# Sixteen gate tiles as seven block products for eight, placed between the quarters of S5, with the gates kept in DRAM

## The chip, the cores and the metric

The kernel runs on one core of a Trainium2 chip. The metric is the device time of one execution in microseconds (us), the median over several runs. Engines: TensorE (PE; matmuls, with its weight loads as PEld), VectorE (DVE), ScalarE (ACT), GpSimd (POOL) and SyncE (SP). SP, ACT and POOL also issue DMA transfers, each through its own queue, and every engine works its instructions off in a fixed order.

## The reference

One decoder layer on x of 1024 tokens by 1024 channels, in float32. An S5 branch and an mLSTM branch read the same normalised x; gates from x weigh them, and their sum goes through a projection. Cross-attention and a gated FFN follow, which the change leaves alone.

```python
h  = rmsnorm(x, g)
u, q, k, v, o, i, f, gates = split(h @ w_in, IN_WIDTHS)   # gates: 2*D_MODEL = 2048 columns
ys = s5(u, ...)                                          # [1024, 512]
ym = mlstm(q, k, v, o, i, f, ...)                        # [1024, 512]
g  = sigmoid(gates + b_gate)
x  = x + (g[:, :D] * (ys @ w_br[0]) + g[:, D:] * (ym @ w_br[1])) @ w_out
# then cross-attention over 256 memory tokens, then the gated ConvFFN, then the last rmsnorm
```

## The kernel before, in words

Activations lie transposed: channels on the 128 partitions, 1024 tokens along a row. A float32 product is made of three float32r products: each factor is split into a high part (a cast on ACT, L186) and a low part (a subtraction on DVE, L187), and `gemm_part` (L214) does high by high, high by low and low by high. `ntile` loads one 512 KB block of weights for 128 output channels through SP's queue (WR), splits it (WH, WL) and runs 8 blocks of 128 channels by 3 products by 2 halves of the tokens, 48 matmuls of 128x512, into a PSUM tile M. A branch tile has 4 blocks of channels, 24 matmuls. `hx` holds the split x, scaled by the norm's gain; the norm's factor per token, `rb`, is multiplied in behind a product.

The order of the work is a list of steps by hand, `ORDER`, run through the loop `for step in ORDER`: `p`, `r` are the parameters and the run of a quarter of S5 (`s5_run`: transfers from Ud and Kd, L546 products, scans on DVE, L582/L583 products, L592 transposes, the result to Yd), `v` and `g` values and gate rows of the mLSTM, `j` a head's projections, `m` a head (`mlstm_head`; L731 to L774 are its products, its last step a power on POOL, L786, and transposes, L793), `s` splits a head's result (`ym_split`), `y` loads an S5 quarter, Gelu and split (`y_load`), `a` one gate tile and one branch tile of the mLSTM side. After the list come the glu tiles, the S5 side's gate and branch tiles (i=0), and then w_out. Instructions are placed by a scheduler that keeps to the data and the free buffers, so that filler from a neighbour step can stand between another step's instructions on PE.

`gate_tile(i, n)` is one `ntile` on `hx`, then a multiplication by `rb` (L800) and a sigmoid (L801); the tile gt lies in R, of which there are four buffers (`NR = 4`); rb holds one of them throughout. `merge_tile` multiplies it with the branch tile. `quad_sums(dst, src, jj, ...)` prepares the sums of weight blocks for products of the seven-for-eight kind that come later: on POOL's queue four DRAM-to-DRAM copies (L850), paced by the matmul that was last when the code was written out, and four adding transfers (L853), of which the third waits for the first, and the fourth for the third. `down_sums` (Dd) comes after every second S5 merge tile, `up_sums` (Uq) after `a5` and `a7` and later. `rstd_col(msq, D, rm)` behind w_out raises to a power on POOL (L242); PE uses rm at L1003. `psM`, `psA` give PSUM tiles M and A.

## Time and profile before

| what | value |
|---|---|
| median of three runs | 1622.83 us (1622.62 to 1624.99) |
| profiled execution | 1622.69 us, span 1620.9 us |
| mean granted clock of PE | 0.996 |
| DMA, mean | 144 GB/s; 233.83 MB |
| L800, DVE, 16 gate tiles | 19.6 us busy, 1222 ns each |
| L801, ACT, the sigmoids | 1154 ns each |
| gate weights, WR from w_in, 512 KB | 3.3 us to landing |

In a group's row of the profile stand line, engine, operation, output and inputs, shape and count; then the busy time, the mean of one in ns, the idle time of the engine just ahead and what ended it. In a row of a timeline the first two numbers are start and length in us, and the bracket gives the idle time ahead. In a row of waits stand the waiting engine, operation and line, what it waited for, the total in us, how often, and the longest.

### The profile page before, as it was taken

The page shows a single profiled execution, that of the slowest core. Times are in us where ns is not written, and L with a number is a line of the kernel's source. Part 1 is how long each engine was busy: PE and PEld are TensorE (multiplying, and loading weights), DVE is VectorE, ACT ScalarE, POOL GpSimd, SP SyncE. Part 2 cuts the span into 40 slices and gives each one's busy share as a digit, 9 for nine tenths or more (in the row PEclk, how much of TensorE's full clock was granted, in tenths as well). Part 3 has the DMA queues.
Part 4 walks back from the last instruction along what each step waited for, and adds up shares of the span by engine and source line. Part 5 has one row for each costly group of instructions (what it writes and reads, how often), then busy time and mean ns, then how long its engine had stood idle before and what let it go on. Part 6 is the DMA issues. An engine that isn't in the chain of part 4 may idle for free.

```text
span 1620.9 us, 20862 instructions
## 1 busy us (share of the span) xinstructions
PE 1597.7 (99%) x8031; PEld 1347.7 (83%) x8031; DVE 1056.6 (65%) x1698; ACT 700.7 (43%) x1153; POOL 144.1 (9%) x216
## 2 busy tenths in 40 slices
PE   9999999999999999999999999999999999999997
PEld 7898888888888888888888888888887888888887
DVE  7878767675344434344466468788889878867535
ACT  6446545633432223343354346444434445543423
POOL 0000000000111112100000000000111011221014
PEclk9999999999999999999999999999999999999998
DMA  5231211313665688953205244532677375886312
GB/s 198 95 97 57 79 53 59 86 46 104 175 156 149 161 252 240 292 132 107 97 29 206 104 156 163 198 108 78 190 183 196 109 181 172 309 284 207 119 39 105
DMA packets 87653, 233.83 MB, mean 144 GB/s; under 512 B 9601, under 2 KB 23617, under 8 KB 87553
## 3 DMA queue, kind: packets, MB, share of 16 engines
q1 hardware_dynamic: 58528, 138.73, 25.7%
q0 software_dynamic: 21488, 75.25, 18.7%
q10 hardware_dynamic: 7536, 18.52, 3.1%
q8 instruction: 63, 1.03, 0.3%
q14 instruction: 38, 0.30, 0.1%
HBM read 201.53 MB, written 85.46 MB: 177 GB/s over the span
## 4 chain that ended last, share of the span: by engine, by line
PE 93%; DVE 2%; issue 1%; DMA 1%; ACT 1%; SPq 0%; POOL 0%; POOLq 0%; DVEq 0%; ACTq 0%
PE M L214 41%; PE A L1208 14%; PE M L1208 10%; PE M L1352 6%; PE A L1352 5%; PE A L214 4%; PE M L299 1%; PE A L1074 1%; PE A L1020 1%; PE A L994 1%; PE M L614 1%; PE M L616 1%; PE M L615 1%; PE A L299 1%; DMA S<-in_w_up_dram 1%
## 5 line engine op out<-in xcount | busy, mean ns | idle before, releaser
L214 PE MATMUL M<-S,WH 128*128 128x512 f32 (+1 forms) x1704 | 459.6, 382 | 1.9 <-DVE dc L787 1.4
L214 PEld LDWEIGHTS M<-S,WH 128*128 128x128 f32 x1704 | 312.9, 188 | 63.0 <-issue 2.1
L214 PE MATMUL M<-S,WL 128*128 128x512 f32 (+1 forms) x884 | 277.5, 381 | 0.0
L186 ACT CAST WH<-WR 128x1024 fp32r<-128x1024 f32 (+2 forms) x107 | 99.4, 930 | 326.6 <-PE M L214 246.9
L214 PEld LDWEIGHTS M<-S,WL 128*128 128x128 f32 x884 | 165.8, 188 | 31.5 <-DVE WL L187 0.5
L187 DVE TENSOR_TENSOR WL<-WR,WH 128x1024 fp32r<-128x1024 f32 (+2 forms) x107 | 114.7, 1072 | 74.9 <-ACT WH L186 73.6
L1208 PE MATMUL M<-S,Y 128*128 128x512 f32 x468 | 112.2, 389 | 0.8 <-DVE Z L1221 0.8
L1208 PEld LDWEIGHTS M<-S,Y 128*128 128x128 f32 x468 | 87.8, 188 | 19.3 <-DVE Z L1221 1.1
L1231 DVE SCALAR_TENSOR_TENSOR S<-Z,cols,S 128x1023 f32<-128x1023 f32 (+1 forms) x72 | 90.8, 1278 | 7.2 <-ACT S L1229 7.2
L1208 PE MATMUL M<-S,W 128*128 128x512 f32 x324 | 78.3, 389 | 0.0
L186 ACT CAST W<-Y 128x512 fp32r<-128x512 f32 x51 | 31.4, 620 | 97.4 <-PE A L1208 67.4
L800 DVE TENSOR_TENSOR R<-M,R 128x1024 f32<-128x1024 f32 x16 | 19.6, 1222 | 82.6 <-PE M L214 82.6
L1208 PEld LDWEIGHTS M<-S,W 128*128 128x128 f32 x324 | 60.8, 188 | 12.6
L1208 PE MATMUL A<-S,W 128*128 128x512 f32 x288 | 70.6, 389 | 0.0
L1208 PEld LDWEIGHTS A<-S,W 128*128 128x128 f32 x288 | 54.1, 188 | 11.2
L1208 PE MATMUL A<-S,Y 128*128 128x512 f32 x240 | 60.1, 389 | 0.0
L1352 PE MATMUL M<-S,W 128*128 128x512 f32 x240 | 57.8, 389 | 0.0
L1208 PE MATMUL A<-R,W 128*128 128x512 f32 x228 | 56.5, 391 | 0.6 <-ACT Z L1215 0.5
L187 DVE TENSOR_TENSOR S<-S,S 128x512 fp32r<-128x512 f32 x79 | 51.8, 683 | 5.9 <-ACT S L186 5.8
L186 ACT CAST S<-S 128x512 fp32r<-128x512 f32 x79 | 46.4, 618 | 17.4 <-PE M L1352 6.1
L214 PE MATMUL A<-S,WH 128*128 128x512 f32 (+1 forms) x184 | 53.2, 372 | 0.5 <-ACT WH L186 0.5
L1208 PE MATMUL A<-VV,W 128*128 128x512 f32 x216 | 53.4, 389 | 0.0
(478 smaller groups left out, 3042.1 us busy)
## 6 DMA issues: line engine op xcount, KB each, us to landing
WR<-in_w_in_dram SPq DMA_DIRECT2D x29, 512.0 KB, 3.3
Uq<-in_w_uq_dram POOLq DMA_DIRECT2D x24, 512.0 KB, 9.0
Dd<-in_w_dq_dram POOLq DMA_DIRECT2D x24, 512.0 KB, 7.5
Td<-Gq POOLq DMA_DIRECT2D x24, 512.0 KB, 8.4
Gq<-S SPq DMA_DIRECT2D x18, 512.0 KB, 3.8
WR<-in_w_o_dram SPq DMA_DIRECT2D x16, 512.0 KB, 3.4
Y<-Uq SPq DMA_DIRECT2D x32, 256.0 KB, 3.9
S<-Td POOLq DMA_DIRECT2D x16, 512.0 KB, 5.4
```

The costliest lines, as they stand in the source:

```text
L186: A.copy(out=hi, in_=src)
L187: (lo_eng or V).tensor_tensor(out=lo, in0=src, in1=hi.bitcast(F32), op=ALU.subtract)
L214: last_mm[0] = PE.matmul(ps[:, s:e], lhsT, rhs[:, s:e], start=first and is_first, stop=last and is_last)
L299: PE.matmul(pus[j][h.start // 512], w_[:, 0, j * P : (j + 1) * P], x_[:, h], start=k == 0 and f, stop=k == KD - 1 and l)
L614: PE.matmul(ps, xh, wh, start=k == 0, stop=False)
L615: PE.matmul(ps, xh, wl, start=False, stop=False)
L616: PE.matmul(ps, xl, wh, start=False, stop=k == KD - 1)
L800: V.tensor_tensor(out=gt, in0=ps, in1=rb, op=ALU.mult)
L994: PE.matmul(pv[2 * m + j], lhsT, rhs[:, 0, 512 * j : 512 * j + 512], start=k == 0 and f, stop=k == KD - 1 and l)
L1208: up_mm[0] = PE.matmul(ps, lhsT[:, c], rhs, start=f, stop=l, skip_group_check=True)
L1231: V.scalar_tensor_tensor(out=acc[:, d_:], in0=raw[:, : T - d_], scalar=col("fcw", 3 * ct + 2 - d_), in1=acc[:, d_:], op0=ALU.mult, op1=ALU ...
L1352: paced[0] = PE.matmul(dps[p][n], lhsT[:, c], rhs, start=f, stop=l, skip_group_check=True)
```

## The change

Each group g of gates now covers four gate tiles (two of either side). Their 2x2 blocks of weights, the 2x2 blocks of x (even and odd blocks of channels, first and second half of the tokens) give seven products instead of eight. `gate_job(p, g)` does product p for group g, 24 matmuls; steps `e<p><g>` in ORDER. Products 2 and 3 are added on in the PSUM tile of the product that is ahead in their group (1 and 5, `gps[g]`); gu and gv keep partial results in VV and S. Weight sums are four `quad_sums` into Gw after `j0` to `j3`. The sums of x are `x_sums`: early (`A`, for product 6) and late (`B`, for 5, 7 and 4): xT is loaded again on POOL's queue into R, scaled on ACT, added on POOL (2 or 5 additions of 128x512) and split. A finished quarter goes through L800's multiplication and a sigmoid into DRAM `Gt` (ACT's queue), and `merge_tile` loads it again (SP's queue). The mLSTM result goes to DRAM `Ym` likewise and comes back in `ym_split`, now the last steps of the list. After the glu tiles the two sides' branch tiles alternate, 24 matmuls each.

```diff
@@ -48,14 +48,14 @@
 NPD = 9
 NPP = (NPD + 1) // 2
 NE = 8
-UP_SUMS_AT = ("a5", "a7")
 ORDER = (
-    "p0 r0 v0 p1 v1 g0 p2 r1 j0 m0 j1 m1 j2 m2 p3 s0 j3 m3 s1 s3 s2 y0 a0 a1 r2 a2 a3 r3 a4 y1 "
-    "y2 y3 a5 a6 a7 "
+    "p0 r0 v0 p1 v1 g0 p2 r1 j0 m0 j1 m1 j2 m2 p3 j3 m3 A0 A1 A2 A3 "
+    "e10 e11 e20 e21 r2 e12 e13 e22 e23 e60 e61 r3 B0 B1 B2 B3 e62 e63 "
+    "e70 e71 e72 e73 y0 y1 e40 e41 e42 e43 y2 y3 e50 e51 e30 e31 e52 e53 e32 e33 s0 s1 s2 s3 "
 ).split()
+GATE_SUMS_AT = {"j0": 0, "j1": 1, "j2": 2, "j3": 3}
+UP_SUMS_AT = {"e71": 0, "e52": 1}
 QKV = (
@@ -199,7 +199,10 @@
         else:
             hi, lo = alloc(F32R)[:, :fw], alloc(F32R)[:, :fw]
         wcount[0] += 1
-        split(hi, lo, raw, low[wcount[0] % 2])
+        if factor is None:
+            split(hi, lo, raw, low[wcount[0] % 2])
+        else:
+            scaled_split(raw, factor, hi, lo)
         return (hi.rearrange("p (k n) -> p k n", k=shape[0]),
                 lo.rearrange("p (k n) -> p k n", k=shape[0]))
@@ -302,6 +305,7 @@
     rb = R()
     Ud = dr.tile([GROUPS, CHG, BLK * NBLK], F32, name="Ud")
     Yd = dr.tile([4, P, T], F32, name="Yd")
+    Ym = dr.tile([NH, P, T], F32, name="Ym")
     Kd = dr.tile([GROUPS, CHG, 7 * CHG + P], F32, name="Kd")
     for j in range(4):
         if j == 3:
@@ -792,20 +796,89 @@
             for c in range(4):
                 PE.transpose(pt[:, c * P : (c + 1) * P], ch(sot, 4 * i + c), ident)
             A.activation(out=ymt[i], in_=pt, func=AF.Copy, scale=col("m_g", h))
-        return ymt
-    def gate_tile(i, n):
-        ps = ntile(a["w_in"][13 + 8 * i + n], hx)
+            A.dma_start(out=Ym[h, :, 512 * i : 512 * i + 512], in_=ymt[i])
+    ngain = cp.tile([P, KD], F32, name="ngain")
+    G.tensor_scalar(out=ngain, in0=col("mix_g", 0, KD), scalar1=-1.0, scalar2=None, op0=ALU.mult)
+    Gw = dr.tile([4, P, 4, T], F32, name="Gw")
+    Gt = dr.tile([2 * KD, P, T], F32, name="Gt")
+    GW = {1: 0, 2: 2, 4: 3}
+    GS = {5: 0, 7: 1, 6: 2, 3: 3}
+    gx = {p: [None] * 4 for p in range(1, 8)}
+    gps, gu, gv = {}, {}, {}
+    def x_sums(late, i):
+        xe, xo = R(), R()
+        G.dma_start(out=xe, in_=a["xT"][2 * i])
+        A.activation(out=xe, in_=xe, func=AF.Copy, scale=col("mix_g", 2 * i))
+        w = slice(0 if late else 512, T)
+        G.dma_start(out=xo[:, w], in_=a["xT"][2 * i + 1][:, w])
+        A.activation(out=xo[:, w], in_=xo[:, w], func=AF.Copy, scale=ngain[:, 2 * i + 1 : 2 * i + 2])
+        def add(out, x, y):
+            G.tensor_tensor(out=out, in0=x, in1=y, op=ALU.add)
+        def put_x(p, v):
+            t = S(F32R)
+            gx[p][i] = t[:, :512], t[:, 512:]
+            split(*gx[p][i], v)
+        e0, e1, o0, o1 = xe[:, :512], xe[:, 512:], xo[:, :512], xo[:, 512:]
+        if not late:
+            add(e0, e0, e1)
+            add(e0, e0, o1)
+            put_x(6, e0)
+            return
+        add(e0, e0, e1)
+        put_x(5, e0)
+        add(e1, e1, o1)
+        put_x(7, e1)
+        add(o0, o0, o1)
+        add(o0, o0, e0)
+        put_x(4, o0)
+    def gate_done(g, b, h, c, src, sign):
+        cv = c.rearrange("p (q t) -> p q t", q=2)
+        V.tensor_tensor(out=cv, in0=src.rearrange("p (q t) -> p q t", q=2),
+                        in1=rb[:, 512 * h : 512 * h + 512].unsqueeze(1).broadcast_to([P, 2, 512]), op=ALU.mult)
+        for q in range(2):
+            A.activation(out=cv[:, q], in_=cv[:, q], func=AF.Sigmoid, scale=sign, bias=col("b_gate", 4 * g + 2 * q + b))
+        A.dma_start(out=Gt[4 * g : 4 * g + 4].rearrange("(q b) p t -> b p q t", b=2)[b, :, :, 512 * h : 512 * h + 512], in_=cv)
+    def gate_job(p, g):
+        src = a["w_gq"][g, :, GW[p]] if p in GW else Gw[g, :, GS[p]]
+        wh, wl = load_w(src.unsqueeze(1), (1, T), factor=-1.0 if p == 3 else None)
+        if p not in (2, 3):
+            gps[g] = psM()
+        ps = gps[g]
+        for q in range(2):
+            for i in range(4):
+                c = slice(512 * q + P * i, 512 * q + P * i + P)
+                xh, xl = gx[p][i]
+                for w, x, f, l in ((wh, xh, i == 0 and p not in (2, 3), False), (wh, xl, False, False), (wl, xh, False, i == 3)):
+                    last_mm[0] = PE.matmul(ps[:, 512 * q : 512 * q + 512], w[:, 0, c], x, start=f, stop=l, skip_group_check=True)
+        if p == 1:
+            gu[g] = VV()[:, :T]
+            A.copy(out=gu[g], in_=ps)
+        elif p == 2:
+            gate_done(g, 0, 0, R(), ps, 1.0)
+        elif p == 6:
+            V.tensor_tensor(out=gu[g], in0=gu[g], in1=ps, op=ALU.subtract)
+        elif p == 7:
+            gv[g] = S()
+            V.tensor_tensor(out=gv[g], in0=gu[g], in1=ps, op=ALU.add)
+        else:
+            c = R()
+            V.tensor_tensor(out=c, in0=(gu if p == 3 else gv)[g], in1=ps, op=ALU.add)
+            gate_done(g, *{4: (1, 0), 5: (1, 1), 3: (0, 1)}[p], c, c, 1.0 if p == 5 else -1.0)
+    merged, mgs = [], []
+    def merge_tile(i, n, ys):
         gt = R()
-        V.tensor_tensor(out=gt, in0=ps, in1=rb, op=ALU.mult)
-        A.activation(out=gt, in_=gt, func=AF.Sigmoid, bias=col("b_gate", 8 * i + n))
-        return gt
-    merged, mgs = [], []
-    def merge_tile(i, n, ys, gt=None):
-        gt = gt or gate_tile(i, n)
+        nc.sync.dma_start(out=gt, in_=Gt[8 * i + n])
         pb = ntile(a["w_br"][i, n], ys, nk=4)
         if i == 1:
             merged.append([Y(), Y()])
@@ -823,20 +896,20 @@
         mgs.append((hi, lo))
-    prm, hp, ym, ymf, ysp = {}, {}, {}, {}, {}
+    prm, hp, ym, ysp = {}, {}, {}, {}
     def ym_split(h):
+        y = Z()
+        nc.sync.dma_start(out=y, in_=Ym[h])
         hi, lo = S(F32R), S(F32R)
-        for i in range(2):
-            hs = slice(512 * i, 512 * i + 512)
-            split(hi[:, hs], lo[:, hs], ymf[h][i])
+        split(hi, lo, y)
         ym[h] = (hi, lo)
     def y_load(j):
         y = Z()
         nc.sync.dma_start(out=y, in_=Yd[j])
         A.activation(out=y, in_=y, func=AF.Gelu_apprx_tanh)
-        hi, lo = (VV(F32R)[:, :T], VV(F32R)[:, :T]) if j < 2 else (S(F32R), S(F32R))
+        hi, lo = S(F32R), S(F32R)
         split(hi, lo, y)
         ysp[j] = (hi, lo, y)
@@ -860,6 +933,10 @@
     def up_sums(g):
         quad_sums(Uq, a["w_uq"], g, (1, 0, 0, 2), (3, 1, 0, 2), last_mm[0])
+    for i in range(4):
+        for p, k, h in ((1, 2 * i, 0), (2, 2 * i + 1, 0), (3, 2 * i + 1, 1)):
+            gx[p][i] = tuple(t[:, 512 * h : 512 * h + 512] for t in hx[k])
     for step in ORDER:
         i = int(step[1])
@@ -874,19 +951,23 @@
         elif step[0] == "j":
             hp[i] = proj_head(i)
         elif step[0] == "m":
-            ymf[i] = mlstm_head(i, *hp[i])
+            mlstm_head(i, *hp[i])
         elif step[0] == "s":
             ym_split(i)
         elif step[0] == "y":
             y_load(i)
+        elif step[0] in "AB":
+            x_sums(step[0] == "B", i)
         else:
-            merge_tile(1, i, [ym[h] for h in range(NH)])
-            if step in UP_SUMS_AT:
-                up_sums(UP_SUMS_AT.index(step))
+            gate_job(i, int(step[2]))
+        if step in GATE_SUMS_AT:
+            quad_sums(Gw, a["w_gq"], GATE_SUMS_AT[step], (1, 0, 0, 2), (3, 1, 0, 2), last_mm[0])
+        if step in UP_SUMS_AT:
+            up_sums(UP_SUMS_AT[step])
     ysp = [ysp[j] for j in range(4)]
-    early = [gate_tile(0, 0)]
+    ym = [ym[h] for h in range(NH)]
     y2 = []
     for j in range(4):
         ps = ntile(a["w_glu"][j], ysp, nk=4)
@@ -898,9 +979,12 @@
             V.tensor_tensor(out=y_, in0=y_, in1=ps[:, hs], op=ALU.mult)
             split(hi[:, hs], lo[:, hs], y_)
         y2.append((hi, lo))
-    early.append(gate_tile(0, 1))
+    merge_tile(1, 0, ym)
+    merge_tile(1, 1, ym)
     for n in range(KD):
-        merge_tile(0, n, y2, early[n] if n < 2 else None)
+        merge_tile(0, n, y2)
+        if n + 2 < KD:
+            merge_tile(1, n + 2, ym)
         if n % 2:
             down_sums(n // 2)
@@ -1594,7 +1678,9 @@
     o = {}
     o["xT"] = c(np.asarray(inp["x"])[0].T.reshape(KD, P, T))
     o["memT"] = c(np.asarray(inp["mem"])[0].T.reshape(2, 4, P, 256).transpose(0, 2, 1, 3))
-    sel = np.concatenate([w_in[:, 384:1536], w_in[:, 2048:2560], w_in[:, 2568:4616]], axis=1)
+    sel = np.concatenate([w_in[:, 384:1536], w_in[:, 2048:2560]], axis=1)
+    wg = w_in[:, 2568:4616].reshape(4, 2, P, 4, 2, 2, P).transpose(3, 2, 1, 5, 4, 0, 6)
+    o["w_gq"] = c(wg.reshape(4, P, 4, T))
     o["w_in"] = ntiles(sel)
     o["w_u"] = c(w_in[:, :384].reshape(KD, P, 384))
     vif = np.concatenate([w_in[:, 1536:1792], w_in[:, 2560:2564], w_in[:, 1792:2048], w_in[:, 2564:2568]], axis=1)
```

Three places in the order. The names are tiles with a running number; M and A are PSUM, S, Z, Y, R, VV buffers of SBUF.

PE in the last head, m3, before: L758 to L774 are the head's steps, L214 a gate tile of another step.

```order
L758 MATMUL A_2899<-S_2713,S_2776 128x128 x4
L765 MATMUL A_2907<-ident,S_2838 128x128 x4
L765 MATMUL A_2913<-ident,S_2838 128x128 x4
L772 MATMUL A_2920<-VV_114,Y_2841 128x129 x2
L774 MATMUL A_2920<-Z_2863,Y_2842 128x129
L214 MATMUL M_3103<-S_240,WH_3099 128x512 x2
L214 MATMUL M_3103<-S_241,WH_3099 128x512 x2
L214 MATMUL M_3103<-S_240,WL_3100 128x512 x2
L214 MATMUL M_3103<-S_276,WH_3099 128x512 x2
```

The same steps in the change (L762 is L758 before, L769 is L765, L776/L778 are L772/L774; L861 is `gate_job`'s matmul):

```order
L762 MATMUL A_2930<-S_2742,S_2805 128x128 x4
L762 MATMUL A_2936<-S_2742,S_2805 128x128 x4
L769 MATMUL A_2944<-ident,S_2867 128x128 x4
L769 MATMUL A_2950<-ident,S_2867 128x128 x4
L776 MATMUL A_2957<-VV_114,Y_2878 128x129 x2
L778 MATMUL A_2957<-Z_2900,Y_2879 128x129
L776 MATMUL A_2965<-VV_115,Y_2878 128x129
L778 MATMUL A_2965<-Z_2900,Y_2879 128x129
L776 MATMUL A_2965<-VV_115,Y_2878 128x129
```

The head's steps follow one another to the last L778 with no matmul of another tile between; e20 begins behind it.

PE at S5's last run, r3, before (L583/L582 its products, M_3724 a gate tile on hx):

```order
L214 MATMUL M_3724<-S_312,WH_3720 128x512 x2
L214 MATMUL M_3724<-S_313,WH_3720 128x512 x2
L214 MATMUL M_3724<-S_312,WL_3721 128x512
L583 MATMUL A_3568<-Y_2645,Y_3558 128x128
L582 MATMUL A_3568<-Z_3491,Z_3490 128x128
```

In the change e70 (M_3772) and e71 (M_3805) stand there, on the summed x (S_3637, S_3656, S_3675 are product 7's x blocks 0 to 2; the fourth is S_3694):

```order
L861 MATMUL M_3772<-S_3637,WH_3768 128x512 x2
L861 MATMUL M_3772<-S_3637,WL_3769 128x512
L861 MATMUL M_3772<-S_3656,WH_3768 128x512 x2
L861 MATMUL M_3772<-S_3656,WL_3769 128x512
L861 MATMUL M_3805<-S_3637,WH_3801 128x512 x2
L861 MATMUL M_3805<-S_3637,WL_3802 128x512
L861 MATMUL M_3805<-S_3656,WH_3801 128x512 x2
L861 MATMUL M_3805<-S_3656,WL_3802 128x512
L861 MATMUL M_3772<-S_3675,WH_3768 128x512
L861 MATMUL M_3805<-S_3675,WH_3801 128x512
L587 MATMUL A_3590<-Y_2680,Y_3580 128x128
L586 MATMUL A_3590<-Z_3513,Z_3512 128x128
```

The tile ahead of r3's products reads a sum made by `x_sums` instead of hx, and the two jobs advance block by block together.

POOL behind the last head's power (L786), before:

```order
L786 TENSOR_TENSOR dc_2919<-dc_2919,mhalf 128x8
L850 DMA Uq<-in_w_uq_dram 128x1024 x4
L853 DMA Uq<-in_w_uq_dram 128x1024 x2
L853 DMA Uq<-Uq 128x1024 x2
L850 DMA Uq<-in_w_uq_dram 128x1024 x4
L853 DMA Uq<-in_w_uq_dram 128x1024 x2
```

In the change (L790 is that power, L814/L817 the loads of x, L821 the additions, L923/L926 `quad_sums`):

```order
L821 TENSOR_TENSOR R_3665<-R_3665 128x512
L821 TENSOR_TENSOR R_3683<-R_3683 128x512
L821 TENSOR_TENSOR R_3665<-R_3665,R_3664 128x512
L817 DMA R_3684<-in_xT_dram 128x1024
L821 TENSOR_TENSOR R_3683<-R_3683,R_3684 128x512
L821 TENSOR_TENSOR R_3684<-R_3684 128x512
L821 TENSOR_TENSOR R_3684<-R_3684,R_3683 128x512
L923 DMA Uq<-in_w_uq_dram 128x1024 x4
L926 DMA Uq<-in_w_uq_dram 128x1024 x2
L926 DMA Uq<-Uq 128x1024 x2
L923 DMA Uq<-in_w_uq_dram 128x1024 x4
```

Eight loads and twenty additions of `B` now lie between the last head's power and the first Uq sum. The two Uq sums, the five Dd sums and two more Uq sums then follow up to rm's power in the order that they had.

More of the change, by code (lines that the diff above doesn't have):

```diff
@@ L190, in hybrid_layer, with load_w @@
     low = [V, V]
-    def load_w(src, shape, alloc=None):
+    def load_w(src, shape, alloc=None, factor=None):
         fw = shape[0] * shape[1]
```

## The prediction

> **What bounds the kernel now.** I read the engines' shares first, then the waits of TensorE (PE), then the chain that ended last, then the stretches of 50 us around the change.
>
> ```profile
> span 1620.9 us, 20862 instructions
> PE 1597.7 (99%) x8031; PEld 1347.7 (83%) x8031; DVE 1056.6 (65%) x1698; ACT 700.7 (43%) x1153; POOL 144.1 (9%) x216
> ...
> PE 93%; DVE 2%; issue 1%; DMA 1%; ACT 1%; SPq 0%; POOL 0%; POOLq 0%; DVEq 0%; ACTq 0%
> ```
>
> PE works 99% of the span. Whatever takes matmuls away is paid out in full, unless PE then waits for something that it does not wait for today. Today it hardly waits between 300 and 700 us, where the change lies:
>
> ```profile
> PE M L214 <- DVE dc L787: 1.4, 1, 1.4
> ...
> PE A L582 <- DMA Z<-Kd: 1.1, 1, 1.1
> ```
>
> ```profile
> 429.38 265.27 PE M L214 x1169
> ```
>
> The columns of the last row are start, length and what ran: 1169 matmuls of the 128x512 form follow one another for 265.27 us without a gap, 0.2269 us each. That is the price of a matmul here. The stretches show what lies beside it (columns: stretch, length, busy us of PE, PEld, DVE, ACT, POOL, granted clock, share of the DMA engines, GB/s):
>
> ```profile
> 350.00:400.00 50.00, 48.95 (x263) 41.16 (x262) 33.88 (x63) 13.90 (x18) 0.00 (x0) 1.00 0.31 100
> ...
> 500.00:550.00 50.00, 50.00 (x222) 41.41 (x221) 21.20 (x30) 12.16 (x15) 9.79 (x15) 1.00 0.78 200
> 550.00:600.00 50.00, 50.00 (x223) 41.39 (x222) 21.26 (x29) 12.54 (x15) 8.30 (x13) 1.00 0.71 187
> 600.00:650.00 50.00, 50.00 (x222) 41.42 (x221) 21.03 (x30) 14.97 (x22) 10.76 (x16) 1.00 0.89 256
> 650.00:700.00 50.00, 49.96 (x220) 41.05 (x220) 25.33 (x42) 19.65 (x35) 7.90 (x11) 1.00 0.99 276
> ```
>
> The granted clock is 1.00, so the matmul price will hold. But from 600 us the DMA engines are nearly full: PE has covered that stretch exactly, and less PE work beside the same bytes uncovers it.
>
> **Matmuls.** Sixteen tiles of 48 are 768; seven products by four groups by 24 are 672. 96 fewer at 0.2269 us: -21.8 us. The two waits above (2.5 us) sit at places that the new waits below replace, so they are taken out here and not counted again: -24.3.
>
> **m3 without filler: +10.** Before, the gate and branch tiles stand between the steps of the last mLSTM head. Rows of PE at its first and its last step, and the foreign matmuls in that stretch:
>
> ```profile
> 295.31 1.09 PE L731 MATMUL A<-ident,S 128*128 128x128 f32 x8
> ...
> 317.08 0.39 PE L774 MATMUL A<-Z,Y 128*128 128x129 f32 x2
> ```
>
> ```profile
> L214 PE MATMUL M<-S,WH 128*128 128x512 f32 x38 | 10.7, 398 | 0.0
> L214 PE MATMUL M<-S,WL 128*128 128x512 f32 x19 | 5.9, 390 | 0.0
> ```
>
> From 295.31 to 317.46 are 22.1 us; 59 foreign matmuls stand between (57 by the groups of 298 to 318, nearly the same stretch), 13.4 us of it, and 8.7 is the head's own. In the new order no matmul of another tile stands between L749 and the last L778. Each step there waits for an eviction of the step ahead. If the head's latency is the 22.1 that it had, PE waits 13.4; if the filler made it that long, PE waits less, down to 0. I take 10, near the top: ACT now has the scalings of A0 to A3 ahead of the head's copies and Exp, DVE their splits, and followed through the two queues by hand the head ends some 31 us after j3 instead of 21.5.
>
> **The sums of x before e70: +17.** B0 to B3 load eight 512 KB tiles of xT on POOL's queue into R, which has four buffers, one of them rb. Gates of e20 to e23 hold the other three until their stores land. Each tile is scaled on ACT, added on POOL, split on ACT and DVE; only then comes the next load. Rows for these (form, count, busy us, mean ns; then two transfers with their us to landing):
>
> ```profile
> L186 ACT CAST WH<-WR 128x1024 fp32r<-128x1024 f32 x79 | 83.0, 1052 | 281.1 <-PE M L214 206.6 <-issue 36.1 <-PE A L214 15.9
> L186 ACT CAST S<-S 128x512 fp32r<-128x512 f32 x79 | 46.4, 618 | 17.4 <-PE M L1352 6.1 <-PE A L1352 2.6 <-DVE S L187 2.2
> ...
> L187 DVE TENSOR_TENSOR S<-S,S 128x512 fp32r<-128x512 f32 x79 | 51.8, 683 | 5.9 <-ACT S L186 5.8
> ```
>
> ```profile
> L1547 POOL TENSOR_TENSOR Z<-Z,Y 128x512 f32<-128x512 f32 x7 | 9.1, 1295 | 61.6 <-ACT Y L1543 61.2
> ...
> S<-Td POOLq DMA_DIRECT2D x16, 512.0 KB, 5.4
> ...
> X1d<-S ACTq DMA_DIRECT2D x8, 512.0 KB, 6.7
> ```
>
> The trace has no such chain, so I bound it. One pair with idle engines: load 5.4, scale 1.05, two adds 2.6, split 1.3, together 10.35; four pairs 41.4, after the store of e22 (6.7): 48.1, less 2.6 as the last pair needs no x4: 45.5 us after e22's end. PE gets there after e23, e60, e61, e62 and e63 (five jobs, 120 matmuls, 27.2), the first three quarters of e70 and e71 (36, 8.2) and S5's own groups in r2 and r3, one round of which shows in these rows of before:
>
> ```profile
> 377.45 1.97 PE L546 MATMUL A<-Z,Y 128*64 128x128 f32 x32
> ...
> 399.38 0.38 PE L583 MATMUL A<-Y,Y 128*128 128x128 f32 x2
> ...
> 402.28 0.39 PE L583 MATMUL A<-Y,Y 128*128 128x128 f32 x2
> ```
>
> With L582/L583 (399.38 to 402.43, 3.05) and the transposes that is about 6: 41.4. So 4 us is the low end. With the queues as the order has them (ACT's scale of the first xo behind weight casts and S5's copies, DVE's splits behind S5's r3 products, which fill 33.88 of 50 us in the like stretch above) the fourth x7 comes at 58.5: 17 us late. Where casts wait a little longer still, 20. I take 17, since the queues are in order and each of those instructions is there.
>
> **The quad sums' tail: +14.0.** Before, POOL issues seven quad sums from the third merge pair on, and the power of rm stands behind the last of them:
>
> ```profile
> 499.87 2.08 POOL L850 DMA_DIRECT2D Dd<-in_w_dq_dram  x4 [31.86 <-PE M L214]
> ...
> 513.02 0.81 POOL L853 DMA_DIRECT2D Dd<-Dd  x1 [4.21 <-DMA Dd<-in_w_dq_dram]
> ...
> 597.72 2.12 POOL L850 DMA_DIRECT2D Dd<-in_w_dq_dram  x4 [11.28 <-PE M L214]
> ...
> 620.50 2.41 POOL L850 DMA_DIRECT2D Dd<-in_w_dq_dram  x4
> ...
> 643.63 2.30 POOL L850 DMA_DIRECT2D Uq<-in_w_uq_dram  x4
> ...
> 670.36 0.81 POOL L853 DMA_DIRECT2D Uq<-Uq  x1 [6.48 <-issue]
> 673.96 2.07 POOL L850 DMA_DIRECT2D Uq<-in_w_uq_dram  x4 [2.79 <-PE M L214]
> ...
> 702.27 0.81 POOL L853 DMA_DIRECT2D Uq<-Uq  x1 [9.62 <-issue]
> 707.17 0.71 POOL L242 TENSOR_TENSOR rm<-ms,mhalf 128x2 f32<-128x2 f32 x1 [4.10 <-DVE ms L241]
> ```
>
> The brackets tell what POOL waited for: up to 597.72 it waited some 11 us for PE before each sum; from 620.50 on the sums run back to back. From the first sum's start to rm were 207.3 us. In that time PE did six gate and six branch tiles of i=0 (6 x 16.34 = 98.1) and then 109.2 us of the w_out stage. Now it does ten branch tiles of 24 matmuls (54.5) there, so rm's power is wanted after 163.6 us. The seven sums back to back, at the lengths of before: four of 22.8 (620.50 less 597.72), 23.1, 27.5 (643.63 to the end of its last issue at 671.17) and 29.1 (673.96 to 703.08): 170.9 us, so 7.3 late. By bytes: the four stretches from 500 to 700 had 168.5 us of full DMA, some 3 more to 707; the same bytes plus about 3.1 MB net (ten gates read back and four branch weights more, six gate weights less) at 3.5 us per MB (0.89 of 50 us for 256 GB/s) are 10.9 more: 182.4 us, 184.2 at a share of 0.99: 20.6 late. It could also be 0, if sums in the emptier part last less. I take the middle of the two counts, 14.0. POOL is then late for r2's power too, and PE waits at L1087 (L1003 before).
>
> **Edits that cost nothing.** The Gw sums stand ahead of the heads' dc power on POOL:
>
> ```profile
> 207.72 1.64 POOL L786 TENSOR_TENSOR dc<-dc,mhalf 128x8 f32<-128x8 f32 x1 [87.18 <-DVE dc L785]
> ```
>
> ```profile
> 214.85 1.04 PE L793 MATMUL A<-ident,Y 128*128 128x128 f32 x8
> ```
>
> Its third step is issued 13.2 us after a sum's start (513.02 less 499.87), and POOL was idle 87 us here, so the power moves by 1 to 3 us; the transposes that need it come 7.1 us later (214.85), of which the power and two DVE steps take some 3.5. Without that cover each of three heads would cost up to 3. Gate stores, 16 on ACT's queue, and 16 reads of Gt and 4 of Ym on SP's land in 5 to 7 us (rows above) against a tile's 5.4 us of PE with two or three tiles of lead; if that goes, the branch tile's eviction and then PSUM is late. The Yd loads behind Gelu at e72 could cost 0 to 3; taken as 0.
>
> **The sum.** The profiled execution took 1622.69 us with its span of 1620.9, 0.1 below the median. 1622.7 - 24.3 + 10 + 17 + 14.0 = 1639.4.
>
> **Rivals.**
>
> *The covers hold (faster).* m3 at 4, B at its 4, no tail: 1622.7 - 24.3 + 8 = 1606. For it: POOL waits 11 us before each sum up to 597.72, so there is air. Against: nothing fills m3 any more. It decides while the three waits stay below 21 together.
>
> *No tail (about the same).* m3 and B as forecast, no sum longer than the fourth: 6 x 22.8 + 23.1 is 159.9, under 163.6, and the time 1639.4 - 14.0 = 1625.4. For it: only the last two were longer, in the fullest stretch. Against: the 0.99 of 650 to 700, whose bytes all remain. It decides where a Uq sum takes 24.6 or less.
>
> *POOL's adds hold up DVE (slower still).* The change puts 28 adds on POOL beside DVE's splits. Near the end of the program both do that today:
>
> ```profile
> 1594.40 6.51 POOL L1565 TENSOR_TENSOR S<-S,Y 128x512 f32<-128x512 f32 x5 [3.18 <-ACT Y L1558]
> ```
>
> ```profile
> 1598.39 2.80 DVE L1547 TENSOR_TENSOR Z<-Z,Y 128x256 f32<-128x256 f32 x2
> ...
> 1603.53 0.95 DVE L1547 TENSOR_TENSOR Z<-Z,Y 128x256 f32<-128x256 f32 x2 [0.22 <-ACT Y L1543]
> ```
>
> POOL's five adds kept their 1.3 us each; two DVE adds of SBUF with SBUF took 2.80 beside them and 0.95 without: 0.9 lost per DVE add. Twenty adds of B (26 us) lie in the 43 us in which DVE owes some 20 such splits and S5 products; half of them hit, 9 us, all on B's chain: 1648. The Trainium skill, "SBUF — State Buffer", section "Who interferes with whom", says that a DVE instruction with two SBUF inputs and a GpSimd instruction that reads SBUF exclude each other for a whole instruction. The trace agrees (0.9 us lost each); by that rule the time would be the rival's. Against it as the likeliest: the splits' lateness is partly in my 58.5 already.
>
> **Chances.** Forecast 0.45, no tail 0.20, covers hold 0.25, adds hold up DVE 0.10. Range 1602 to 1652: below it lies the quarter of the covers' case in which nothing waits (1598.4), above it little more than the slow ends together (m3 13.4, B 20, tail 20.6 would be 1652.4). The forecast's own range is 1630 to 1652. A measurement here tells about 0.2%, 3.2 us, from no change. Faster takes the covers case and a quarter of no tail: 0.30; the same, half of no tail and a little of the forecast's low end: 0.12; slower the rest, 0.58.
>
> **What the changed profile would show.** PE with 96 fewer matmuls and three new rows among its waits: in m3 (DVE or ACT, A tiles, 10 us in pieces), at e70 (waiting for the split of x7, about 17 in four pieces), and at L1087 for POOL's rm (about 15, with the last Uq accumulate just ahead on POOL). If PE is 99% busy again, the covers held and I am wrong; if it waits where I named no wait (the gate reads, psM, weights), the cause is another.

## The result: 3.2% slower, 1676 us

The changed kernel takes 1676.06 us (median of four runs, 1672.66 to 1678.82) against 1623.3 for the kernel before beside it: 1.0322 times the time, 95% interval 1.0299 to 1.0346. The prediction was 1639.4, its range 1602 to 1652. The direction was right, the size was not. All times here are medians of fast executions; three slow ones of two of the kernels below (1762, 2682 and 4107 us) are left out.

The page of the changed kernel, its first lines (the span, then busy time and share of each engine):

```profile
span 1670.6 us, 21041 instructions
PE 1601.9 (96%) x7935; PEld 1346.0 (81%) x7935; DVE 1111.9 (67%) x1742; ACT 739.5 (44%) x1210; POOL 207.4 (12%) x289
```

PE runs 96 instructions fewer (8031 to 7935), as it should, yet it is busy 4.2 us longer (1597.7 to 1601.9). At 0.2269 us per matmul 21.8 us should have gone, to 1575.9; so the remaining matmuls cost 26.0 us more than before. The rest of the span, in which PE stands still, grew from 23.2 to 68.7, by 45.5. Together: -21.8 + 26.0 + 45.5 = 49.7, the difference of the two spans. The bytes that the DMA engines moved grew as well, from 233.83 to 285.21 MB. Where the time lies is seen in the stretches (length, busy us of PE, PEld, DVE, ACT, POOL, granted clock, DMA share, GB/s):

```profile
300.00:350.00 50.00, 34.03 (x213) 29.27 (x213) 29.76 (x55) 26.95 (x56) 11.59 (x12) 0.80 0.79 215
350.00:400.00 50.00, 44.54 (x242) 36.89 (x239) 33.44 (x50) 27.49 (x35) 8.44 (x9) 0.97 0.56 165
400.00:450.00 50.00, 33.85 (x134) 25.70 (x134) 32.10 (x43) 23.31 (x29) 19.52 (x19) 0.76 0.48 164
...
700.00:750.00 50.00, 47.00 (x195) 37.75 (x194) 23.24 (x39) 18.28 (x35) 10.75 (x16) 0.93 0.95 274
750.00:800.00 50.00, 44.32 (x228) 37.93 (x227) 15.50 (x23) 11.96 (x18) 3.17 (x3) 0.93 0.36 101
```

PE idles in three places: m3 (16.0 us of 300 to 350), S5's last runs and e60 to e71 (5.5 and 16.2 of 350 to 450), and rm's place (3.0 and 5.7 of 700 to 800). The granted clock, 1.00 there before, falls to 0.80, 0.76 and 0.93 in the same stretches. The waits of PE (total, times, longest):

```profile
PE M L861 <- ACT S L186: 7.9, 2, 5.5
PE A L508 <- ACT Y L503: 7.5, 1, 7.5
PE M L861 <- DVE VV L868: 7.1, 2, 4.1
PE A L749 <- DVE Y L736: 6.1, 2, 6.0
PE A L1087 <- POOL rm L245: 5.4, 1, 5.4
PE M L861 <- DVE WL L187: 3.2, 2, 2.1
PE M L861 <- ACT WH L186: 2.5, 1, 2.5
PE M L217 <- ACT S L269: 2.5, 2, 1.9
```

How much of the 26.0 is the clock is seen where it was granted by half. Between 300 and 800 us there are seven such spells; two of them and the sum of all seven (columns as above):

```profile
310.51:327.57 17.06, 8.62 (x63) 7.59 (x64) 5.09 (x9) 10.18 (x19) 6.65 (x7) 0.50 1.01 254
...
412.91:429.98 17.07, 10.48 (x27) 6.71 (x28) 12.51 (x21) 3.20 (x4) 6.79 (x7) 0.50 0.63 215
...
sum 61.44, PE 41.44 PEld 33.03 DVE 32.10 ACT 28.86 POOL 19.57; mean PE 5.92 PEld 4.72 DVE 4.59 ACT 4.12 POOL 2.80
```

PE works 41.44 us in them at half speed, so 20.7 us are lost to the clock, in a stretch where the kernel before has 1.00 throughout. A pair of matmul groups inside a spell shows the price (timeline: start, length, what):

```profile
763.43 1.05 PE L1078 MATMUL A<-WL,S 128*128 128x512 f32 x2
764.29 0.95 PE L1078 MATMUL A<-WH,S 128*128 128x512 f32 x3
```

The second group starts 0.86 us after the first, whose two 128x512 matmuls so took 0.43 each; 0.2269 is the price at full clock. The other 5.3 of the 26.0 lie outside these spells and stay unexplained.

### The profile page after: what moved, and what is told of

Its sections match the earlier page's. It is cut to its first block, busy times and chain, and to the rows that moved or that the text cites. A ratio compares the mean times of both kernels' runs of the same rounds, so it can differ in the third digit from the quotient of the medians.

```text
span 1670.6 us, 21041 instructions
## 1 busy us (share of the span) xinstructions
PE 1601.9 (96%) x7935; PEld 1346.0 (81%) x7935; DVE 1111.9 (67%) x1742; ACT 739.5 (44%) x1210; POOL 207.4 (12%) x289
## 2 busy tenths in 40 slices
DMA packets 104420, 285.21 MB, mean 171 GB/s; under 512 B 11264, under 2 KB 25280, under 8 KB 104320
## 4 chain that ended last, share of the span: by engine, by line
PE 52%; issue 1%; DVE 1%; POOL 0%; ACT 0%; DMA 0%; POOLq 0%; DVEq 0%
PE A L1292 14%; PE M L1292 11%; PE M L217 9%; PE M L1436 6%; PE A L1436 4%; PE A L217 4%; PE A L1158 1%; PE A L1104 1%; PE A L1078 1%; PE A L1145 0%; ACT WH L186 0%; DVE Z L1631 0%; POOL S L1649 0%; DVE WL L187 0%; DVE mx L1106 0%
## 5 line engine op out<-in xcount | busy, mean ns | idle before, releaser
L217 PE MATMUL M<-S,WH 128*128 128x512 f32 (+1 forms) x1224 | 331.7, 381 | 3.7 <-ACT S L269 2.5
L186 ACT CAST WH<-WR 128x1024 fp32r<-128x1024 f32 (+2 forms) x115 | 107.7, 938 | 285.9 <-PE M L217 138.4
L217 PE MATMUL M<-S,WL 128*128 128x512 f32 (+1 forms) x644 | 204.1, 380 | 0.1
L187 DVE TENSOR_TENSOR WL<-WR,WH 128x1024 fp32r<-128x1024 f32 (+2 forms) x115 | 126.4, 1100 | 82.1 <-ACT WH L186 80.6
L861 PE MATMUL M<-S,WH 128*128 128x512 f32 x448 | 145.0, 404 | 17.6 <-ACT S L186 7.9
L861 PEld LDWEIGHTS M<-S,WH 128*128 128x128 f32 x448 | 86.5, 195 | 38.1 <-ACT S L186 8.9
L861 PE MATMUL M<-S,WL 128*128 128x512 f32 x224 | 90.2, 403 | 3.2 <-DVE WL L187 3.2
L861 PEld LDWEIGHTS M<-S,WL 128*128 128x128 f32 x224 | 43.4, 194 | 13.5 <-DVE WL L187 5.0
## 6 DMA issues: line engine op xcount, KB each, us to landing
Uq<-in_w_uq_dram POOLq DMA_DIRECT2D x24, 512.0 KB, 10.3
```

Source lines behind the costliest of these rows:

```text
L186: A.copy(out=hi, in_=src)
L187: (lo_eng or V).tensor_tensor(out=lo, in0=src, in1=hi.bitcast(F32), op=ALU.subtract)
L217: last_mm[0] = PE.matmul(ps[:, s:e], lhsT, rhs[:, s:e], start=first and is_first, stop=last and is_last)
L861: last_mm[0] = PE.matmul(ps[:, 512 * q : 512 * q + 512], w[:, 0, c], x, start=f, stop=l, skip_group_check=True)
```

## What an idle PE costs: the kernel before, with six waits put in

The changes of code, here and below, are shown shortened.

```diff
+        if n in (2, 3): hold[0] = evict[n - 2]            # the gate tile's L800, L801
+        else: ACT copies a 128x512 tile 2, 5, 9 or 17 times behind the gate tile; hold[0] = the last
         pb = ntile(a["w_br"][i, n], ys, nk=4)              # its first matmul waits for hold[0]
```

> The kernel before, with six waits put in: the branch tiles (0,2) to (0,7) may start only when something behind the gate tile ahead is done: its multiplication on DVE (n=2), its sigmoid on ACT (n=3), or 2, 5, 9, 17 copies of 128x512 on ACT behind that (n=4 to 7). The output stays the reference's. PE should stand still for about 1.5, 2.6, 3.9, 5.7, 8.2 and 13 us, 35 in all, in a stretch where it never waits today. Theory clock (an idle PE is granted half the clock for some us when it starts again): behind the longer waits a matmul takes 0.43 us instead of 0.227 for 3 to 5 us, behind the shortest none; the time rises by 35 and 2 us more for each of four or five waits, 43 to 47. Theory traffic (the slow matmuls of the changed kernel come from its DMA or DVE load): all matmuls stay at 0.227, the time rises by 35.

Measured: 1669.7 us, 46 more than the kernel before (1.0277, interval 1.0247 to 1.0307). PE's timeline, the first matmuls behind each of the six waits, and some that follow (L804 and L805 are L800 and L801 in this run, L818 the copies):

```profile
512.40 1.16 PE L215 MATMUL M<-S,WH 128*128 128x512 f32 x4 [1.41 <-DVE R L804]
513.85 1.07 PE L215 MATMUL M<-S,WH 128*128 128x512 f32 x4
...
531.47 2.07 PE L215 MATMUL M<-S,WH 128*128 128x512 f32 x4 [2.50 <-ACT R L805]
533.34 1.05 PE L215 MATMUL M<-S,WL 128*128 128x512 f32 x2
534.20 1.35 PE L215 MATMUL M<-S,WH 128*128 128x512 f32 x4
...
553.42 2.07 PE L215 MATMUL M<-S,WH 128*128 128x512 f32 x4 [3.80 <-ACT Y L818]
...
578.25 2.07 PE L215 MATMUL M<-S,WH 128*128 128x512 f32 x4 [5.75 <-ACT Y L818]
...
605.23 2.07 PE L215 MATMUL M<-S,WH 128*128 128x512 f32 x4 [8.34 <-ACT Y L818]
...
637.56 2.08 PE L215 MATMUL M<-S,WH 128*128 128x512 f32 x4 [13.54 <-ACT Y L818]
639.44 1.05 PE L215 MATMUL M<-S,WL 128*128 128x512 f32 x2
640.29 1.24 PE L215 MATMUL M<-S,WH 128*128 128x512 f32 x4
```

Four matmuls take 1.07 us at full clock and 2.07 at half. After 1.41 us of idling nothing changes. After each of the five longer waits the clock is halved, and PE works 3.3, 5.3, 4.3, 4.6 and 3.0 us at half speed, no longer behind 13.54 us of idling than behind 2.50. PE stood still 33.3 us more than before and was busy 13.5 more (1611.2 against 1597.7), with the same matmuls and no DMA added. Half of the 20.5 us of slow work is 10.3, about 2.1 for each of the five; another 1.7 is a half-speed spell at 756.65, ahead of which PE shows no wait, and whose cause is open. Theory clock held, theory traffic fell. So such a wait costs itself and about 2 us behind it, and a wait in pieces can pay each time.

The run doesn't give a sharp limit, though. The same eight transposes behind m3's last wait, first in the changed kernel, then in the one without B (below):

```profile
330.94 1.96 PE L769 MATMUL A<-ident,S 128*128 128x128 f32 x8 [2.39 <-DVE Y L763]
```

```profile
330.25 1.09 PE L769 MATMUL A<-ident,S 128*128 128x128 f32 x8 [2.64 <-DVE Y L763]
```

They run at half speed behind 2.39 us and at full speed behind 2.64. In the profiles compared here every wait of 3 us or more had half-speed work behind it, and no lone wait under 1.8 did; between them it went either way (1.81 without B halved the clock, 1.84 in the changed kernel did not). In every one of these traces the changes of the clock lie a whole number of 3.413 us apart (the starts 310.51 and 412.91 above are 102.40 apart, 30 times that), and where that grid lies against the program differs from execution to execution; that a short wait has to fall well on the grid would explain the two rows, but no run tested it. A few us of the difference between two profiles can be chance of this kind.

The Trainium skill, "TensorE: Matmul & The Clock Gate", section "What's actually happening", describes a gate that halves the clock after an idle window of about 3.4 us and frees it after a busy one. The trace agrees with that length, as the half-speed spells last 3.41 us or a multiple of it (17.07 above); the idle time that set them off could be less, 1.81 to 2.50 us.

## Who held PE: the sums of x, the sums of weights, the late start

Five runs take pieces out or move them, each timed beside the kernel before. Without A:

```diff
+        if not late:
+            gx[6][i] = gx[1][i]
+            return
```

> The changed kernel without the early sums A: product 6 multiplies the x blocks of product 1 instead (the gates are then others; the matmuls are as many). Theory queue (in m3 the head's copies stand on ACT's queue behind scalings that wait for xT loads): the waits at L508 (7.5) and L749 (6.0) go, with the slow matmuls behind them some 15 to 22 us, to 1654-1661. Theory latency (a head without filler waits for its own evictions): the waits move within the head and less than 5 us is gained, above 1670.

Measured: 1661.95 us (1.0229, 1.0198 to 1.0261), 14 less than the changed kernel, just under the least that theory queue gave and far more than theory latency allows. But the waits did not go: PE stands still 69.6 us in the profiled execution, against 68.7, and at L508 8.8 us against 7.5; two new waits are 5.3 at L762 and 5.0 for DVE's L982. What of A costs the 14 us is not shown by this trace. ACT in the changed kernel, at the place where PE waits (brackets: idle time ahead and what ended it):

```profile
311.26 1.15 ACT L815 ACTIVATE R<-R,cols 128x1024 f32<-128x1024 f32 x1 [3.70 <-DMA R<-in_xT_dram]
312.31 1.00 ACT L503 COPY Y<-S 64x64 f32<-64x64 f32 x4
...
318.96 1.15 ACT L815 ACTIVATE R<-R,cols 128x1024 f32<-128x1024 f32 x1 [4.90 <-DMA R<-in_xT_dram]
320.01 0.25 ACT L516 COPY Y<-A 128x128 f32<-128x128 f32 x1
```

ACT stands before a scaling of A whose load has not landed, and L503 (for L508) and L516 (for L749, through DVE) stand behind it. The transfers of the changed kernel between 295 and 325 us (issues, size, median us to landing):

```profile
R<-in_xT_dram POOLq DMA_DIRECT2D x2, 512.0 KB, 14.2
```

My prediction had 5.4 us for such a load. The two took 13.0 and 15.4 beside the last Gw sum, with the DMA engines full (share 1.01 from 310.51 to 327.57, above), so the full engines have their part in this wait too, and no run parts them from the queues.

Without A, in the same place, ACT and POOL:

```profile
316.18 1.02 ACT L503 COPY Y<-S 64x64 f32<-64x64 f32 x4 [5.76 <-POOL Y L499]
```

```profile
315.00 0.82 POOL L929 DMA_DIRECT2D Gw<-Gw  x1 [10.91 <-DMA Gw<-in_w_gq_dram]
315.53 0.62 POOL L499 MEMSET Y<- 128x256 f32 x1
```

Now L503 waits 5.76 us for a memset on POOL, and the memset stands behind the third step of the last Gw sum, which waited 10.91 us for its transfer. PE waits at L508 no less than before (8.8), for another queue. The memset belongs to S5's last parameters; on POOL no row of my prediction looked at it.

Without B:

```diff
+        if late:
+            gx[5][i], gx[7][i], gx[4][i] = gx[1][i], gx[2][i], gx[3][i]
+            return
```

> The changed kernel without the late sums B: products 5, 7 and 4 multiply the x blocks of products 1, 2 and 3 instead (other gates, as many matmuls). Theory chain (PE waits at e60 to e71 for the x sums and for what they hold up on ACT and DVE): the waits between 388 and 440 us (21 us in the trace) go, with their slow matmuls 25 to 32 us, to 1644-1651. Theory S5 (DVE is full of S5's work there anyway): only the two waits for the split itself go, 8 us and their slow spells, about 1662.

Measured: 1646.17 us (1.0145, 1.0114 to 1.0175), 30 less than the changed kernel: theory chain. It is the largest piece. PE idles 13.9 us less (1641.8 - 1587.0 = 54.8 against 68.7) and is busy 14.9 less (1587.0 against 1601.9) with as many matmuls: here the slower matmuls took as much as the waits. PE works 25.6 us at half clock in this trace and 48.3 in the changed kernel's, so 11.3 of the 14.9 are the clock's.

The Dd sums two branch pairs earlier:

```diff
+        if n % 2 == 0:
+            down_sums(n // 2)
         merge_tile(0, n, y2)
...
-        if n % 2:
-            down_sums(n // 2)
```

> The changed kernel with each of the five Dd sums issued two branch pairs earlier (paced by the merge tiles ahead of an even n, not behind an odd n). Theory queue (POOL comes late to rm's power as the sums start too late): the wait at L1087 (5.4), those for the residual's loads (3.0) and the slow matmuls behind go, 8 to 13 us, to 1663-1668. Theory bytes (the DMA engines are full from 560 to 757 us, so the last sum ends when the bytes are through): the gain is under 3 us.

Measured: 1663.02 us (1.0241, 1.0217 to 1.0265), 13 less: theory queue. POOL in the changed kernel, from the first Dd sum to rm, and then with the sums earlier:

```profile
580.51 2.08 POOL L923 DMA_DIRECT2D Dd<-in_w_dq_dram  x4 [42.14 <-PE M L217]
...
606.07 2.36 POOL L923 DMA_DIRECT2D Dd<-in_w_dq_dram  x4
...
757.40 0.81 POOL L926 DMA_DIRECT2D Uq<-Uq  x1 [8.14 <-issue]
757.94 1.01 POOL L245 TENSOR_TENSOR rm<-ms,mhalf 128x2 f32<-128x2 f32 x1
```

```profile
746.61 0.81 POOL L926 DMA_DIRECT2D Uq<-Uq  x1 [6.54 <-issue]
747.15 1.01 POOL L245 TENSOR_TENSOR rm<-ms,mhalf 128x2 f32<-128x2 f32 x1
```

From 580.51 to 757.94 are 177.4 us, seven sums without a pause from 606 on, and rm's power follows at once where it had 4.10 us of air before. With the sums earlier, POOL starts the first at 556.96, 23.6 us sooner, but rm's power comes only 10.8 sooner: the seven then take 190.2 us, at a DMA share of 0.91 to 1.00 from 590 to 740. So about half of the head start is lost again, as theory bytes would have it. Of the 11 us between the two profiled spans, some 4 are clock in stretches that this edit doesn't touch.

Without A, B and the Gw sums, and then also with the Dd sums earlier:

```diff
+        gx[6][i] = gx[5][i] = gx[1][i]
+        gx[7][i], gx[4][i] = gx[2][i], gx[3][i]
+        return
...
-        src = ... if p in GW else Gw[g, :, GS[p]]
+        src = ... if p in GW else a["w_gq"][g, :, GS[p]]
...
-        if step in GATE_SUMS_AT: quad_sums(Gw, ...)
```

> The changed kernel without the x sums A and B and without the four Gw weight sums (products read other blocks of x and of the weights: other gates, the same 672 matmuls, the gates still go through DRAM). Theory queues (each wait in m3 and at e60 to e71 is an engine's queue held by an instruction that waits for a DMA of the sums): m3 waits under 5 us in all, nothing at e60 to e71, and only the tail at L1087 is left, 5 to 8 and its slow matmuls: 1610 to 1620, faster than before. Theory filler (a head without other matmuls between its steps waits for its own evictions whatever the queues hold): m3 still waits 10 us or more, with half-speed matmuls behind, 1622 to 1632.

> The same with the five Dd sums two branch pairs earlier. Theory queues: the tail is gone too, 6 to 12 us less than without the move, 1602 to 1612; this is what the 96 matmuls saved are worth when nothing waits (1598 to 1601 by my prediction's first term). Theory bytes (the DMA engines limit the stretch up to rm): under 3 us less.

Measured: 1626.3 us (1.0019, 1.0006 to 1.0032) and 1620.31 us (0.9974, 0.9956 to 0.9992). PE's waits of the first that belong to this stretch:

```profile
PE M L864 <- ACT WH L186: 5.9, 1, 5.9
PE A L749 <- DVE Y L736: 3.8, 1, 3.8
PE A L1088 <- POOL rm L245: 3.3, 1, 3.3
...
PE A L508 <- ACT Y L503: 1.5, 1, 1.5
```

L508 fell from 7.5 to 1.5: with neither A on ACT nor the Gw sum on POOL ahead, that wait is gone, so the two queues, with the transfers that they waited for, were its cause. L749 keeps 3.8. Its multiplication on DVE (L736) stands behind one (L725) that waited 1.81 us for a load from Rd, so a queue has part of that as well. In m3 PE waits 6.3 in all, more than the 5 of theory queues and less than the 10 of theory filler; the time is the one that filler gave, but in part for another reason. A weight cast behind PE's products keeps 5.9 at another place; the cast waited 4.89 us for the transfer of its weights, and why that came late stays open. The early Dd sums bring 6 to 7 us (6.0 by the medians, 7.3 by the two ratios), the low end of what theory queues gave, and from a higher start: with none of the sums to make, the 96 matmuls are worth about 4 us (3.1 by the two profiled spans), not 22. By the second run's page (PE busy 1585.1 of 1617.8) 9.5 of it go to idling that the kernel before doesn't have, and 9.2 to matmuls that cost more, 6.1 of that at half clock.

## Does POOL's adding hold up DVE?

The sums of x from the split x in SBUF, without loads and scalings:

```diff
-        G.dma_start(out=xe, in_=a["xT"][2 * i]) ... scale, add
+        acc(v, half(e, 0, 0), half(e, 0, 1)); acc(v, v, half(e, 1, 0)); ...   # 5 adds per A, 10 per B, on POOL
```

> The changed kernel with the x sums made on POOL from the split x that lies in SBUF (hx, high and low parts, 5 adds per A and 10 per B) instead of from xT loaded again and scaled: no transfer and no scaling in A and B; the output is the reference's. Theory queues: ACT's head is no longer held by a load, the waits at e70 shrink to what the splits cost; L508 stays (POOL's memset behind the last Gw sum): 1640 to 1655. Theory port (POOL's adds lock DVE's SBUF adds out): 60 adds instead of 28 take DVE another 20 to 30 us where it is full, no gain or slower, above 1665.

Measured: 1687.72 us (1.0399, 1.0379 to 1.042), 12 more than the changed kernel: theory port. DVE and POOL in one stretch of it:

```profile
308.85 4.92 DVE L187 TENSOR_TENSOR WL<-WR,WH 128x1024 fp32r<-128x1024 f32 x1
```

```profile
309.06 1.55 POOL L817 TENSOR_TENSOR R<-R,S 128x512 f32<-128x512 f32 x1
...
310.87 4.02 POOL L817 TENSOR_TENSOR R<-R,S 128x512 f32<-128x512 f32 x2
```

A weight split that takes 1.22 us takes 4.92 while POOL makes three additions, and POOL's additions take 2.0 instead of 1.3. Each lasts longer beside the other. The kernel as a whole doesn't part this from POOL's own longer chain, sixty additions instead of 28, which the splits of x wait for as well.

In the changed kernel itself the longest weight split between 290 and 460 us takes 2.46. S5's steps on DVE lose more: the same step in r2, and in r3 beside POOL's additions:

```profile
359.12 0.68 DVE L559 TENSOR_TENSOR Y<-Y,Y 128x512 f32<-128x512 f32 x1
...
404.81 1.78 DVE L559 TENSOR_TENSOR Y<-Y,Y 128x512 f32<-128x512 f32 x1
```

```profile
404.27 1.77 POOL L821 TENSOR_TENSOR R<-R,R 128x512 f32<-128x512 f32 x1 [1.43 <-ACT R L818]
```

L560 behind it takes 1.77 instead of 0.68, and the first four scans (L563) 3.47 instead of 1.3: 4.4 us in all. L868, which evicts a gate job's PSUM tile, stands behind them on DVE, and PE waits 4.1 us for it.

With each Gw sum one step earlier and the Dd sums earlier as well:

```diff
-GATE_SUMS_AT = {"j0": 0, "j1": 1, "j2": 2, "j3": 3}
+GATE_SUMS_AT = {"r1": 0, "j0": 1, "j1": 2, "j2": 3}
```

> The kernel with sums from hx, with each Gw sum one step earlier (after r1, j0, j1, j2 instead of j0 to j3) and the Dd sums two branch pairs earlier; the output is the reference's. Theory queues: L508 no longer waits behind the last Gw sum and the tail shrinks: 15 to 25 us less than with hx alone, 1618 to 1635. If it stays above 1645, the queues were not what held m3 and rm.

Measured: 1678.6 us (1.0335, 1.0303 to 1.0367), 9 less than with hx alone. My expectation of 1618 to 1635 missed by 44 us: it left the sixty additions' cost out. By its own sign (above 1645) the queues are not what holds m3 and rm in this kernel; its waits were not read.

The changed kernel with its 28 additions on DVE:

```diff
-            G.tensor_tensor(out=out, in0=x, in1=y, op=ALU.add)
+            V.tensor_tensor(out=out, in0=x, in1=y, op=ALU.add)
```

> The changed kernel with the 28 additions of x sums on DVE instead of POOL; nothing else changes, the output is the reference's. Theory port (an addition on POOL and an operation of DVE with two SBUF inputs lock each other out, and POOL takes 1.3 us where DVE takes 0.6): DVE does the work sooner than it waited for it, 5 to 15 us less, 1660 to 1670. Theory load (DVE is the full engine in this stretch, 17 us more of work on it come on top): no gain or slower, above 1675.

Measured: 1667.96 us (1.0263, 1.0229 to 1.0298), 8 less, though DVE has more to do. The intervals of the two ratios touch at their ends (1.0298 and 1.0299). The weight splits of this stretch, in the changed kernel and with the additions on DVE (shortest, median, longest in ns):

```profile
L187 DVE TENSOR_TENSOR WL<-WR,WH x16: 1192/1216/2458, 295.0 to 454.9; 128x1024 fp32r<-128x1024 f32 x16
```

```profile
L187 DVE TENSOR_TENSOR WL<-WR,WH x17: 1214/1218/1231, 296.5 to 458.1; 128x1024 fp32r<-128x1024 f32 x17
```

No split is late any more, L559 and L560 take 0.69 and 0.68 again in r3, and PE's waits for L868 fall from 7.1 to 3.0. So POOL's additions had their part, and 8 us is near what the prediction's last rival gave them (9). That the whole 8 is the lock-out is not shown: PE stands still as long in the two profiles (68.0 and 68.7), since it waits longer for a split of x (10.5 against 7.9) and for rm (9.6 against 5.4), and the shorter span is shorter by cheaper matmuls.

## More work for PE, and the pieces together

Forty-eight matmuls more, where PE waits:

```diff
+        again = 3 if p == 1 and g == 1 else 1
-            for i in range(4):
+            for i in range(4 * again):
+                i %= 4
```

> The changed kernel with e11's 24 matmuls done three times over (the last time counts, the output is the reference's): 48 matmuls of 128x512 more, 10.9 us of work, of which the order puts 28 ahead of L508 and 20 ahead of L749 in m3. Theory clock: PE stands still there anyway (7.5 and 6.0 us); the work fills the waits, the matmuls behind them are no longer at half speed, and the time does not rise: 0 to 6 us less than the changed kernel, 1668 to 1676. Theory work (what PE has to do sets the time): 10.9 us more, 1685 to 1687.

Measured: 1677.87 us (1.0333, 1.0311 to 1.0354), 1.8 more than the changed kernel, whose runs spread over 6. Of 10.9 us of matmuls about nine cost nothing, so PE's work does not set the time here. The time falls between the two theories, nearer to theory clock, but the saving that this one gave was not seen: PE was busy 10.2 more, and while the wait at L508 went, one of 5.8 came at L762, behind DVE's L755.

The additions on DVE, the Gw sums one step earlier, the Dd sums earlier (the three edits above in one):

> The changed kernel with the additions on DVE, each Gw sum one step earlier (r1, j0, j1, j2) and the Dd sums two branch pairs earlier; the output is the reference's. Theory queues: POOL's memset for p3 is no longer behind the last Gw sum and the tail shrinks as in the kernel with the early Dd sums (13 us there), with what the additions on DVE bring: 1645 to 1660, still slower than before, since A's loads and B's chain stay. If it stays above 1665, the pieces do not add.

Measured: 1650.27 us (1.0162, 1.0143 to 1.0182), 26 less than the changed kernel, as theory queues gave, and still 27 more than the kernel before. Its waits that are left in m3 and behind are 4.8 at L508, 4.4 at L749 and 5.4 for a split of x. No version that was run and computes the reference beats the kernel before.

## Why the prediction was too low

- **Matmuls, -21.8.** The count was right. The price was not: "The granted clock is 1.00, so the matmul price will hold" is the step that failed. I read the clock from a kernel whose PE hardly idles and forecast 41 us of idling beside it. The matmuls left cost 26.0 us more, 20.7 of it at half clock, which the sum put at nothing. With the 26.0 alone added, the sum is 1639.4 + 26 = 1665.
- **m3, +10.** The stretch lost 16.0 to idling, more than the bound of 13.4, but in two parts. The head's own steps waited 8.4 (6.0 at L749, 2.4 at L769), near the row. The other 7.5 came at L508, a product of S5's last parameters ahead of them, which I took for no step of the head: it waits for ACT behind a load that took 13.0 us and, once A's loads are taken out, for POOL's memset. The row's mechanism, a head that has no filler, is only part even of the 8.4, since L516 for L749 stood behind a load too.
- **Sums of x, +17.** PE lost 16.2 in 400 to 450 and 5.5 before. This is the largest piece, as forecast; without B 30 us come back, a good part of it clock. But only 7.9 of it, in two waits, is the one I named, the split of x. 7.1 is L868 on DVE, whose first wait (4.1) follows S5 steps that POOL's additions drew out, and 5.7 are weight casts and splits, one of them (2.5) behind a scaling that waited for xT. These are places that I had written down as signs of another cause (psM, weights). The waits for L868 and for the weight splits all but go without B too, so the piece was right and its inside was not.
- **Quad sums, +14.0.** The wait was 5.4, 3.0 more around 733 for the residual's tiles, so 8.4, near the low count (7.3). That it is so near is partly luck: the seven sums took 177.4 us against the 170.9 I counted, and PE came to L1087 173.1 us after the first sum's start, not 163.6. The mechanism was right: moving the sums earlier gave 13 back, clock included.
- **Edits that cost nothing.** Gate stores and reads and the dc powers hardly showed: 4.0 us of idling from 200 to 300, of which 1.8 and 1.7 at L762. The memset was missing from this list.
- **The rivals.** Covers hold and no tail fell. The port rival is real, with up to 8 us in the changed kernel; I gave it 0.10 and not as an addition to the others, which it was.

The new waits less the two old ones were 38.5 us by my sum (41.0 less 2.5) and 45.5 by the trace, a miss of 7. The range missed because it was the sum of the waits' ends, and no end held the clock.

## What to carry to other kernels

Price every new wait of PE by more than its length: in a kernel bound by PE, a new wait of 3 us or more cost some 2 us of half-speed matmuls on top here, each time; one of about 2 to 3 us did so or not. When a step is moved onto an in-order queue, look for every instruction of other steps behind it on that queue (a memset, a small copy), not only for those of the change, and ask which transfer the instruction ahead waits for. Saved matmuls pay only where the filler that covered other steps' latency remains: here, with all the sums taken out, 21.8 us of work saved were worth 4.

## What the runs showed that I had not expected

- The half-speed work does not grow with the wait: 3.3 us behind 2.5, 3.0 behind 13.5. Waits of 1.81 and 2.39 us set it off, one of 2.64 did not, and the clock changes only on a grid of 3.41 us.
- POOL additions of SBUF tiles and DVE operations with two SBUF inputs slow each other: 1.22 to 4.92 us for a split, 0.68 to 1.78 for an S5 step, 1.3 to 2.0 for an addition.
- A memset of 0.6 us on POOL ended a wait of PE of 8.8 us, since it stood behind a step that waited 10.91 us for its transfer.
